# Projecting the attention branch with seven products in place of eight, and moving the weight sums into the attention heads

## The chip, the cores and the metric

The kernel runs on one core of a Trainium2 chip. The metric is device time in microseconds of one execution. The engines are PE (TensorE: matrix products, with weight loads shown as PEld), DVE (VectorE), ACT (ScalarE), POOL (GpSimd) and SP (SyncE, which here only issues transfers). The profile gives the time of every instruction on every engine.

## The reference

One layer of an encoder trunk on 1,024 rows of 1,024 columns, in float32:

```python
h = rmsnorm(x, g_mix)
z = h @ w_in                      # pooling channels | q | k | v
y_pool = pool_mixer(u_pool, w_pool_grp, pool_scale)            # (S, 512)
y_attn = diff_attention(q, k, v, g_q, g_k, lam, g_sub, ...)    # (S, 1024), 8 heads
gates = sigmoid(h @ w_gate + b_gate)                           # (S, 2048)
merged = (gates[..., :D] * (y_pool @ w_branch_pool)
          + gates[..., D:] * (y_attn @ w_branch_attn))
x = x + merged @ w_out
h2 = rmsnorm(x, g_ffn)
x = x + square(relu(h2 @ w_up)) @ w_down
```

The change concerns the two lines of `merged`, and the loading of weights for them and for `w_out`.

## The kernel before, in words

*Products in three passes.* Every float32 operand is split into a high part (a cast to fp32r on ACT) and a low part (a subtraction on DVE or POOL): `split(hi, lo, src, lo_eng)`, lines 131 and 132 in the profile. `mm3` then issues three matmuls: high x high, high x low, low x high (lines 138 to 140). Almost all matmuls of the kernel are of this kind, with up to 512 moving columns.

*Stages.* First the attention heads. A loop over `g` steps through 64 pairs of a head and a row tile (8 heads of 8 tiles of 128 rows). In one step, each of the stages A (q, k, v projection), B (preparation: norm of q and k), C (transposes), D (scores), E (transposed weights), F (product with v), H and R (norm of the output) works on a different pair, in the order of the string `O`. Stage B uses POOL for the power of the norm (`ms`, line 271) and to scale k (`qn`, line 710). Stage W loads the weights of the next head two steps before it begins, into the two buffers of `raw`, and splits them with POOL. Units of other work fill PE in between: the gate columns (`fwgate`, written to `g_dram`) and the pooling groups (written to `p_dram`). Each head writes its unscaled output to `y_dram` and one scale per row to `r_dram`. The order of the instructions on each engine is made by a scheduler that goes by the order of the program and by estimated times; each engine then works its list in order. All loads shown as SP's are issued from SP's one queue, in order.

*The branch stage.* A first loop over eight column tiles `d` projects the pooling branch (`branch_pool`: 24 matmuls; ACT copies the two halves into `mp[d]`). Beside it the same loop forms sums of blocks of `w_out` on POOL and stores them to DRAM (`w_out_sums`), and loads, scales and splits the attention output (`yT`). A second loop over `d` multiplies `mp[d]` with its gate (`gp`), projects the attention branch with 48 matmuls (`ba`, `proj_T`, both halves, eight depth tiles each), multiplies with the other gate (`ga`, result `mg`), adds it into `mp[d]` on POOL, and begins to make the left operands of the next stage (`a_set`).

*The output projection* multiplies `merged` with `w_out` as a 2 x 2 matrix of blocks by seven products in place of eight (Strassen's scheme in Winograd's form). The weight blocks come from `w_out` and from its sums in DRAM; the sums of the left operand are formed on DVE (`half(...)`). Products accumulate on one another in PSUM, named by digits: `A_RAW` says which half tile each uses. After it, the second norm and the MLP follow, whose two products use the same scheme.

*Buffers.* PSUM has eight banks; in the branch stage `ps_z` has two, `ps_f` one, `pb` five. In SBUF: `up` (tag U, 11 tiles of 128 x 1,024), `vpool` (6), `fwpool` (4), `wpool` (tags W0 and W1, 4 each), `rpool` (2 raw tiles), `fp` (`fr` and `fo`, 2 each), `fq` (one each of `fu`, `mx`), `hp0` (two times 4) and `hp1` (8).

Of the kernel before, what the change touches and what calls it, by code (L numbers as in the profile page):

```python
# [50 lines left out]
F_FROM, F_PACE, F_UNITS = 4, 0.5, 34  # L51

# [11 lines left out]
def encoder_kernel(  # L64
# [101 lines left out]
    def load_cols(src, c0, name, nk=NK):  # L166

        rw = raw([P, nk, P], f"r{name}")
        nc.sync.dma_start(rw, src[0 : nk * P, c0 : c0 + P].rearrange("(kk p) c -> p kk c", p=P))
        ws = []  # L170
        for j in range(0, nk, 4):
            w = wt([P, 2, 4, P], f"w{name}_{j}")
            split(w[:, 0], w[:, 1], rw[:, j : j + 4, :], nc.gpsimd)
            ws.append(w)
        return ws

    def load_cols2(src, c0, name):

        rw = raw([P, 4, 2 * P], f"r{name}")
        nc.sync.dma_start(rw, src[0 : 4 * P, c0 : c0 + 2 * P].rearrange("(kk p) c -> p kk c", p=P))  # L180
        ws = []
        for j in range(2):
            w = wt([P, 2, 4, P], f"w{name}_{j}")
            split(w[:, 0], w[:, 1], rw[:, :, j * P : (j + 1) * P], nc.gpsimd)
            ws.append([w])
        return ws

# [13 lines left out]
    def proj_T(ps, ws, rhs, th, nk=NK):  # L201

        for k in range(nk):
            w = ws[k // 4]
            r_hi, r_lo = rhs(k, th)
            mm3(ps, w[:, 0, k % 4, :], w[:, 1, k % 4, :], r_hi, r_lo, k == 0, k == nk - 1)
        return ps

    def load_split(src, r0, name, tile_fn, scale=None):

        rw = raw([P, S], f"r{name}") if scale is None else wt([P, S], f"r{name}", F32)
        nc.sync.dma_start(rw, src[r0 : r0 + P, :])
        if scale is not None:
            rbs, row = scale
            n = S // len(rbs)
            for i, rb in enumerate(rbs):
                js = slice(i * n, (i + 1) * n)
                nc.sync.dma_start(rb, row[js].partition_broadcast(P))
                nc.vector.scalar_tensor_tensor(rw[:, js], rw[:, js], gs, rb, op0=ALU.mult, op1=ALU.mult)
# [17 lines left out]

    def branch_pool(d, ws, ps_fn):

        m = htile([P, S], F32, f"mp{d}", 1)  # L240
        for th in range(2):
            ps = proj_T(ps_fn(f"bp{d}_{th}"), ws, lambda k, th: pair(ypT[k][th]), th, nk=4)
            nc.scalar.copy(m[:, th * 512 : (th + 1) * 512], ps)
        mp.append(m)
# [21 lines left out]
    yd = dram.tile([S, D], F32, name="yd")  # L266

# [145 lines left out]
    with ExitStack() as ph:  # L413
# [502 lines left out]

        units, made = fillers(), 0
        for g in range(-2, N + 10):
# [10 lines left out]
            if g == G_COLS:  # L929
                columns()  # L930
            gens = {}
# [40 lines left out]
    def yt_tile(d):  # L972
        fn = ut if d < N_YU else vt
        return lambda shape, dt, name, th: fn(shape, dt, name)

# [7 lines left out]
    ws_bp = {0: load_cols2(w_branch_pool, 0, "bp0")}  # L983
    ypT = [load_split(p_dram, g * P, f"ypT{g}", ypt_tile) for g in range(4)]
    mp, yT, ws_ba = [], [], {}
    w_sum = [dram.tile([S // 2, D], F32, name=f"w_sum{i}") for i in range(2)]

    def w_out_sums(d):

        b1, b2 = (vt([P, D], F32, f"wos{d}_{i}") for i in range(2))  # L990
        for i, b in enumerate((b1, b2)):
            nc.sync.dma_start(b, w_out[(d + 4 * i) * P : (d + 4 * i + 1) * P, :])
        (b11, b12), (b21, b22) = ((b[:, 0:512], b[:, 512:D]) for b in (b1, b2))
        sub(pool, b11, b12, b11)
        sub(pool, b12, b22, b12)
        sub(pool, b22, b22, b11)
        sub(pool, b21, b21, b22)
        for i, b in enumerate((b1, b2)):
            nc.sync.dma_start(w_sum[i][d * P : (d + 1) * P, :], b)

    for d in range(NK):
        if d % 2 == 0 and d + 2 < NK:
            ws_bp[d + 2] = load_cols2(w_branch_pool, (d + 2) * P, f"bp{d + 2}")
        elif d > NK - 4:
            j = len(ws_ba)
            ws_ba[j] = load_cols(w_branch_attn, j * P, f"ba{j}")
        branch_pool(d, ws_bp[d - d % 2][d % 2], bank)
        if d < 4:
            w_out_sums(d)
        if d % 4 < 2:  # L1010
            rb = [fu_tile(f"rb{d}") if d % 2 else ut([P, S], F32, f"rb{d}")]
        else:
            rb = [tmp(f"rb{d}_{i}") for i in range(2)]
        yT.append(load_split(y_dram, d * P, f"yT{d}", yt_tile(d), (rb, r_dram[d])))
    def half(d, th):
        return mp[d][:, th * 512 : (th + 1) * 512]

# [6 lines left out]
    a_sets = {}  # L1024
    for d in range(NK):
        if d + 2 < NK:
            ws_ba[d + 2] = load_cols(w_branch_attn, (d + 2) * P, f"ba{d + 2}")
# [7 lines left out]
        for th in range(2):  # L1035
# [5 lines left out]
            if th == 0:  # L1041
                a_set("1" if d < 4 else "2", d % 4)
# [576 lines left out]
```

## Time and profile before

| | |
|---|---|
| runs (median, lowest, highest) | 1529.79, 1528.99, 1529.82 us |
| span of the profiled execution | 1526.9 us |
| its own time | not given apart; the median of the runs is 2.9 us above the span |
| heads | to about 640 us |
| last gate columns | 640 to 695.7 us |
| pooling projection | 695.7 to 739.4 us |
| attention projection | 739.4 to 826.3 us |
| output projection | from 826.3 us |
| transferred | 213.75 MB, mean 140 GB/s |

A row of the groups reads: line, engine, operation, output<-inputs, shapes, xcount | busy us, mean ns of one | idle time of the engine before them, and what ended it. A row of a tile's view reads: line, engine, operation, xcount: shortest/median/longest ns, first and last start. A matmul's duration there is a modelled latency, since matmuls overlap in the array; starts are measured. A row of the waits reads: engine and line <- what ended the wait: us in total, times, longest. A row by stretches has, for each engine, its busy us and the number of its instructions, then the granted clock of TensorE, the busy share of the 16 DMA engines, and GB/s.

### The profile page before, as it was taken

How to read it: one execution, taken by the hardware profiler on the slowest of the kernel's cores; microseconds unless marked ns; L12 is line 12 of the kernel's file. 1: busy time of each engine (PE TensorE's matmuls, PEld its weight loads, DVE VectorE, ACT ScalarE, POOL GpSimd, SP SyncE). 2: the span in 40 equal slices, each digit the busy share in tenths (PEclk: the TensorE clock that was granted, in tenths of full speed). 3: DMA queues.
4: the chain of work that ended last, by engine and by line, in shares of the span. 5: the costliest groups of instructions: out<-in, count | busy, mean ns of one | idle time of the engine just before them, and what ended most of it. 6: DMA issues, size and time to landing. Idle time of an engine off the chain costs nothing.

```text
span 1526.9 us, 21743 instructions
## 1 busy us (share of the span) xinstructions
PE 1517.4 (99%) x7637; PEld 1316.2 (86%) x7637; DVE 1025.5 (67%) x2135; ACT 794.6 (52%) x1653; POOL 389.4 (26%) x466
## 2 busy tenths in 40 slices
PE   9999999999999999999999999999999999999999
PEld 8899999999999999888888887888888788888887
DVE  7877766677777777742645899676656678556672
ACT  6655555556555555544633467565555634333331
POOL 5525242434334352318646510000000000000000
PEclk9999999999999999999999999999999999999999
DMA  6212111111202021339745633554433899537650
GB/s 213 66 48 66 34 53 52 59 51 39 73 31 80 33 87 49 118 106 376 269 139 174 212 138 117 173 195 156 152 124 111 290 333 367 182 125 260 229 191 28
DMA packets 168583, 213.75 MB, mean 140 GB/s; under 512 B 10165, under 2 KB 104090, under 8 KB 168474
## 3 DMA queue, kind: packets, MB, share of 16 engines
q1 hardware_dynamic: 151050, 185.05, 36.4%
q10 hardware_dynamic: 17424, 27.31, 4.9%
q8 instruction: 60, 0.98, 0.3%
q14 instruction: 49, 0.40, 0.1%
HBM read 154.62 MB, written 57.70 MB: 139 GB/s over the span
## 4 chain that ended last, share of the span: by engine, by line
PE 96%; DVE 2%; DMA 1%; ACT 1%; issue 0%; SPq 0%; POOLq 0%; POOL 0%; ACTq 0%; DVEq 0%
PE z L138 6%; PE z L139 5%; PE z L140 5%; PE Da L139 4%; PE Da L140 4%; PE Da L138 4%; PE g L138 4%; PE g L139 4%; PE g L140 4%; PE Db L138 3%; PE Db L139 3%; PE Db L140 3%; PE X L138 3%; PE X L139 3%; PE X L140 3%; PE sc L767 2%
## 5 line engine op out<-in xcount | busy, mean ns | idle before, releaser
L138 PE MATMUL z<-wqkv,hT 128*128 128x384 f32 x512 | 173.7, 340 | 1.2 <-ACT hT L131 1.1
L140 PE MATMUL z<-wqkv,hT 128*128 128x384 f32 x512 | 173.6, 339 | 0.4 <-DVE hT L437 0.3
L139 PE MATMUL z<-wqkv,hT 128*128 128x384 f32 x512 | 173.2, 338 | 0.0
L778 ACT ACTIVATE s<-s,nm 128x256 f32<-128x256 f32 (+7 forms) x128 | 99.5, 778 | 77.6 <-DVE nm L770 74.3
L271 POOL TENSOR_TENSOR ms<-ms,mhalf 128x4 f32<-128x4 f32 x64 | 66.7, 1042 | 186.8 <-DVE ms L270 183.3
L138 PE MATMUL g<-hT,fwgate 128*128 128x512 f32 x256 | 101.0, 395 | 0.0
L139 PE MATMUL g<-hT,fwgate 128*128 128x512 f32 x256 | 100.5, 392 | 0.0
L140 PE MATMUL g<-hT,fwgate 128*128 128x512 f32 x256 | 100.4, 393 | 0.0
L138 PEld LDWEIGHTS z<-wqkv,hT 128*128 128x128 f32 x512 | 96.2, 188 | 4.0 <-ACT hT L131 1.2
L140 PEld LDWEIGHTS z<-wqkv,hT 128*128 128x128 f32 x512 | 96.2, 188 | 2.6 <-DVE hT L437 0.9
L139 PEld LDWEIGHTS z<-wqkv,hT 128*128 128x128 f32 x512 | 96.3, 188 | 2.4 <-DVE wqkv L437 0.3
L770 DVE CUSTOM_DVE_ANT_0 s<-sc,dist 128x512 f32<-128x512 f32 (+3 forms) x128 | 74.1, 585 | 21.2 <-PE sc L768 20.3
L767 PE MATMUL sc<-K,Q 128*128 128x512 f32 (+2 forms) x192 | 67.5, 357 | 0.4 <-DVE nm L770 0.4
L768 PE MATMUL sc<-K,Q 128*128 128x512 f32 (+2 forms) x192 | 66.1, 349 | 0.0
L132 DVE TENSOR_TENSOR AS<-s,AS 128x512 fp32r<-128x512 f32 x64 | 43.4, 687 | 30.9 <-ACT AS L131 30.9
L132 POOL TENSOR_TENSOR wqkv<-rqkv,wqkv 128x384 fp32r<-128x384 f32 x56 | 58.7, 1065 | 14.6 <-ACT wqkv L131 14.2
L132 POOL TENSOR_TENSOR fwgate<-frgate,fwgate 128x512 fp32r<-128x512 f32 x32 | 43.5, 1361 | 66.0 <-ACT fwgate L131 66.0
L140 PEld LDWEIGHTS g<-hT,fwgate 128*128 128x128 f32 x256 | 48.1, 188 | 9.5
L138 PEld LDWEIGHTS g<-hT,fwgate 128*128 128x128 f32 x256 | 48.1, 188 | 9.1 <-ACT go L387 0.2
L139 PEld LDWEIGHTS g<-hT,fwgate 128*128 128x128 f32 x256 | 48.1, 188 | 8.8
L132 DVE TENSOR_TENSOR AT_0l<-ta,AT_0h 128x512 fp32r<-128x512 f32 (+1 forms) x48 | 32.0, 666 | 32.0 <-ACT AT_0h L131 31.7
L139 PE MATMUL ba<-yT,wba 128*128 128x512 f32 x128 | 49.6, 389 | 0.0
(481 smaller groups left out, 4625.9 us busy)
## 6 DMA issues: line engine op xcount, KB each, us to landing
wd<-in_w_down_dram SPq DMA_DIRECT2D x56, 512.0 KB, 5.4
wu<-in_w_up_dram SPq DMA_DIRECT2D x32, 512.0 KB, 4.3
udS<-us SPq DMA_DIRECT2D x64, 256.0 KB, 3.3
ur<-udS SPq DMA_DIRECT2D x32, 512.0 KB, 4.5
rqkv<-in_w_in_dram SPq DMA_DIRECT2D x64, 192.0 KB, 3.0
ur<-ud SPq DMA_DIRECT2D x24, 512.0 KB, 6.4
frgate<-in_w_gate_dram SPq DMA_DIRECT2D x32, 256.0 KB, 3.6
g_dram<-go ACTq DMA_DIRECT2D x32, 256.0 KB, 3.2
```

The lines of the kernel that those rows point to most:

```text
L132: (lo_eng or nc.vector).tensor_tensor(lo, src, f(hi), op=ALU.subtract)
L138: nc.tensor.matmul(ps, lhs_hi, rhs_hi, start=first, stop=False, **kw)
L139: nc.tensor.matmul(ps, lhs_hi, rhs_lo, start=False, stop=False, **kw)
L140: return nc.tensor.matmul(ps, lhs_lo, rhs_hi, start=False, stop=last, **kw)
L271: nc.gpsimd.tensor_tensor(dst, dst, mhalf[:, :n], op=ALU.pow)
L767: nc.tensor.matmul(dst, Q[:, i, 0, :], rhs, start=True, stop=False)
L768: nc.tensor.matmul(dst, Q[:, i, 1, :], rhs, start=False, stop=True)
L770: nc.vector.tensor_tensor_reduce(out=s[i][:, c : c + w], in0=sc[:, 0:w], in1=dist[:, o0 + c : o0 + c + w], scale=2.0 ** -(h + 1), scalar=B ...
L778: nc.scalar.activation(s[i][:, 0:n], s[i][:, 0:n], AF.Exp, bias=last, scale=-1.0, accum_out=Z[:, i, t : t + 1])
```

## The change

- The attention branch is projected by seven products on 2 x 2 blocks (512 x 512), in the order `1265734`, with operands named as in the output projection. The weight blocks come from `w_branch_attn` and from its sums in DRAM; the sums of y are formed on DVE. y is loaded whole and scaled (`load_y`), and split for each product (`by_set`, low part on DVE); the weights are loaded and split for each product (`wa_set`, low part on POOL). Some partial results are copied out of PSUM by ACT, others are added on DVE; `merge` multiplies with the gate on DVE and adds into `mp` on POOL (the last product: on DVE).
- The sums of `w_branch_attn` and `w_out` are formed by POOL during the heads: 16 calls of `weight_sums`, each on 128 x 256 columns of four blocks, in the steps `g` of 8 or more whose remainder by 8 is 1, 3 or 5, ahead of the step's stages. They go through `raw` tiles and SP's queue. The old `w_out_sums` goes.
- The pooling branch (`gated_pool`) loads its gate first; DVE multiplies straight out of PSUM into `mp`, in place of ACT's copy and a later multiplication.
- The column loaders and `proj_T` go; the order of the loads around the branch changes with it.

The diff, without the removed helpers and a few tile functions:

```diff
+SUM_FROM, SUM_T = 8, (1, 3, 5)
...
+    w_sum = {n: [dram.tile([S // 2, D], F32, name=f"{n}_sum{i}") for i in range(2)] for n in "ao"}
...
+        def weight_sums(n, d, c):
+            src, eng = w_branch_attn if n == "a" else w_out, nc.gpsimd
+            r = raw([P, 4, 256], f"ws{n}{d}_{c}")
+            def rows_of(t, d):
+                return t[d * P : (d + 1) * P, :].rearrange("p (j c) -> p j c", j=2)[:, :, c * 256 : (c + 1) * 256]
+            for i in range(2):
+                nc.sync.dma_start(r[:, 2 * i : 2 * i + 2, :], rows_of(src, d + 4 * i))
+            b11, b12, b21, b22 = (r[:, i, :] for i in range(4))
+            def put(op, out_, a, b):
+                eng.tensor_tensor(out_, a, b, op=op)
+            if n == "a":
+                put(ALU.add, b22, b12, b22)
+                put(ALU.subtract, b12, b11, b12)
+                put(ALU.subtract, b11, b22, b11)
+                put(ALU.subtract, b21, b21, b11)
+            else:
...
+            for i in range(2):
+                nc.sync.dma_start(rows_of(w_sum[n][i], d), r[:, 2 * i : 2 * i + 2, :])
+        sums = [(n, d, c) for n in "ao" for d in range(4) for c in range(2)]
...
+            if g % 8 in SUM_T and sums and g >= SUM_FROM:
+                weight_sums(*sums.pop(0))
...
-    def w_out_sums(d):
...
-    for d in range(NK):
-        if d % 2 == 0 and d + 2 < NK:
-            ws_bp[d + 2] = load_cols2(w_branch_pool, (d + 2) * P, f"bp{d + 2}")
-        elif d > NK - 4:
-            j = len(ws_ba)
-            ws_ba[j] = load_cols(w_branch_attn, j * P, f"ba{j}")
-        branch_pool(d, ws_bp[d - d % 2][d % 2], bank)
-        if d < 4:
-            w_out_sums(d)
-        ...
-        yT.append(load_split(y_dram, d * P, f"yT{d}", yt_tile(d), (rb, r_dram[d])))
+    def gated_pool(d):
+        gp = gate_tile(f"gp{d}", d)
+        gate(whole(gp)[0], d)
+        mp.append(htile([P, S], F32, f"mp{d}", 1))
+        w = ws_bp.pop(d)
+        for th in range(2):
+            ps = bank(f"bp{d}_{th}")
+            for k in range(4):
+                mm3(ps, w[:, 0, k, :], w[:, 1, k, :], *pair(ypT[k][th]), k == 0, k == 3)
+            nc.vector.tensor_tensor(half(d, th), ps, gp[:, th * 512 : (th + 1) * 512], op=ALU.mult)
+    def load_y(d):
+        t = ut([P, S], F32, f"yr{d}")
+        nc.sync.dma_start(t, y_dram[d * P : (d + 1) * P, :])
+        for i in range(2):
+            js = slice(i * 512, (i + 1) * 512)
+            rb = tmp(f"rb{d}_{i}")
+            nc.sync.dma_start(rb, r_dram[d][js].partition_broadcast(P))
+            nc.vector.scalar_tensor_tensor(t[:, js], t[:, js], gs, rb, op0=ALU.mult, op1=ALU.mult)
+        yr.append(t)
...
+    B_ORDER = "1265734"
+    def wa_set(j):          # W tiles, tag by the parity of the product's place
...
+            wa[j] += load_rows(
+                src, (d0 + d) * P, dh * 512, f"a{j}_{d}", lambda shape, name: w_tile(shape, name, n % 2)
+            )
+    def by_set(j):
+        n = B_ORDER.index(j)
+        by_[j] = []
+        for d in range(4):
+            t = (fw_tile if n % 2 else lambda shape, name: vt(shape, F32R, name))([P, 2, 512], f"by{j}_{d}")
+            split(t[:, 0, :], t[:, 1, :], BY[j](d))
+            by_[j].append(t)
+    def b_product(ps, j, i):
+        c = slice(i * P, (i + 1) * P)
+        for d in range(4):
+            mm3(
+                ps, wa[j][d][:, 0, c], wa[j][d][:, 1, c], *pair(by_[j][d]),
+                j in "125" and d == 0, d == 3, j not in "125",
+            )
+    def merge(d, th, k, eng):
+        ga = tmp(f"ga{d}_{th}")
+        gate([(ga, th * 512, (th + 1) * 512)], NK + d)
+        out_ = ga if k.space == PSUM else k
+        nc.vector.tensor_tensor(out_, k, ga, op=ALU.mult)
+        add(eng, half(d, th), half(d, th), out_)
...
-    for d in range(NK):
...
-            ps = proj_T(bank(f"ba{d}_{th}"), ws, lambda k, th: pair(yT[k][th]), th)
-            mg = tmp(f"mg{d}_{th}")
-            nc.vector.tensor_tensor(mg, ps, ga[:, hs], op=ALU.mult)
-            add(pool, half(d, th), mg, half(d, th))
...
+    load_bp(0)
     for d in range(NK):
+        if d % 2 == 0 and d + 2 < NK:
+            load_bp(d + 2)
+        gated_pool(d)
+        load_y(d)
+        if d == 3:
+            wa_set("1")
+            by_set("1")
+            for e in range(4):
+                sub(dve, yh(e, 0), yh(e, 1), yh(e, 0))
+    wa_set("2")
+    by_set("2")
+    for d in range(4):
+        sub(dve, t2(d), yh(d + 4, 1), yh(d, 0))
+        sub(dve, yh(d + 4, 0), yh(d + 4, 0), t2(d))
+        sub(dve, yh(d, 1), yh(d + 4, 1), yh(d, 1))
+    X = [pb.tile([P, 512], F32, tag="b", name=f"bX{i}") for i in range(4)]
+    x1 = kept4("bx1")
+    for i in range(4):
+        b_product(X[i], "1", i)
+        nc.scalar.copy(x1[i], X[i])
+    wa_set("6")
+    by_set("6")
+    Y = [o_bank(f"bY{i}", i) for i in range(4)]
+    for i in range(4):
+        b_product(Y[i], "2", i)
+        add(dve, x1[i], Y[i], x1[i])
+        merge(i, 0, x1[i], pool)
+        a_set("1", i)
+    wa_set("5")
+    by_set("5")
+    U2 = kept4("bU2")
+    for i in range(4):
+        b_product(X[i], "6", i)
+        nc.scalar.copy(U2[i], X[i])
+    wa_set("7")
+    by_set("7")
+    Z = [o_bank(f"bZ{i}", i) for i in range(4)]
+    z5 = kept4("bz5")
+    for i in range(4):
+        b_product(Z[i], "5", i)
+        nc.scalar.copy(z5[i], Z[i])
+    wa_set("3")
+    by_set("3")
+    for i in range(4):
+        b_product(X[i], "7", i)
+        add(dve, z5[i], X[i], z5[i])
+        merge(i + 4, 1, z5[i], pool)
+    wa_set("4")
+    by_set("4")
+    for i in range(4):
+        b_product(Z[i], "3", i)
+        add(dve, U2[i], Z[i], U2[i])
+        merge(i, 1, U2[i], pool)
+        add(dve, half(i, 1), half(i, 1), half(i + 4, 1))
+        sub(dve, half(i, 0), half(i, 1), half(i, 0))
+    for i in range(4):
+        b_product(X[i], "4", i)
+        merge(i + 4, 0, X[i], dve)
+        a_set("2", i)
+        sub(dve, half(i + 4, 0), half(i + 4, 0), half(i, 0))
```

More of the change, by code (lines that the diff above doesn't have):

```diff
@@ L164, in fu_tile @@
         return fq.tile([P, S], F32, tag="fu", name=name)
[L166 to L186, printed above, removed]
     loads = {}
```

110 lines of the change are left out of this document (46 added, 64 removed).

## The prediction, made before the changed kernel was run

> **What bounds the kernel now.** I read the page's busy times and chain first, then who PE waited for, then the busy times stage by stage, and last the rows of the two projections.
>
> ```profile
> span 1526.9 us, 21743 instructions
> PE 1517.4 (99%) x7637; PEld 1316.2 (86%) x7637; DVE 1025.5 (67%) x2135; ACT 794.6 (52%) x1653; POOL 389.4 (26%) x466
> PE 96%; DVE 2%; DMA 1%; ACT 1%; issue 0%; SPq 0%; POOLq 0%; POOL 0%; ACTq 0%; DVEq 0%
> ...
> PE z L138 <- ACT hT L131: 1.1, 1, 1.1
> PE sc L767 <- DVE nm L770: 0.4, 1, 0.4
> ```
>
> The third line is the chain: 96% of it is PE. The last two are everything that PE waited for between 40 and 930 us (engine, line, releaser; total us, times, longest). Heads, branch stage and output projection together hold 1.5 us of waiting, so a matmul taken away there is worth its whole time, and any wait put there costs its whole time.
>
> ```profile
> core 0: us, PE busy (x) PEld busy (x) DVE busy (x) ACT busy (x) POOL busy (x), PEclk, DMA share, GB/s
> 120.00:640.00 520.00, 519.55 (x3021) 479.99 (x3020) 377.74 (x1136) 298.32 (x773) 201.62 (x277) 1.00 0.19 59
> 640.00:695.70 55.70, 55.70 (x281) 47.05 (x280) 25.05 (x61) 26.54 (x50) 10.86 (x12) 1.00 0.40 134
> 695.70:739.40 43.70, 43.70 (x194) 36.21 (x193) 16.44 (x16) 19.90 (x36) 38.30 (x28) 1.00 1.04 394
> 739.40:826.30 86.90, 86.90 (x385) 71.94 (x384) 44.41 (x52) 38.06 (x56) 49.91 (x36) 1.00 0.46 144
> 826.30:880.60 54.30, 54.30 (x241) 44.98 (x240) 41.60 (x54) 24.29 (x50) 32.01 (x23) 1.00 0.70 236
> ```
>
> The rows are the heads, the last gate columns, the pooling projection, the attention projection, and most of the output projection. The granted clock is 1.00 throughout. The output projection matters most as a witness: it already runs seven products with the same splits, and PE never waits in it. In the pooling row the DMA engines are full (1.04).
>
> ```profile
> 739.43 0.39 PE L138 MATMUL ba<-yT,wba 128*128 128x512 f32 x1
> ...
> 826.24 0.39 PE L140 MATMUL ba<-yT,wba 128*128 128x512 f32 x1
> L138 PE MATMUL ba<-yT,wba x128: 389/389/389, 739.4 to 825.8; 128*128 128x512 f32 x128
> L1039 DVE TENSOR_TENSOR mg<-ba,ga x16: 676/682/693, 749.8 to 830.1; 128x512 f32<-128x512 f32 x16
> ```
>
> The attention projection is 3 x 128 = 384 matmuls. Their starts run from 739.43 to 826.24 us, 86.81 us for 383 steps: one starts every 0.2267 us. The 389 ns are a latency, not a price.
>
> **The change, part by part.**
>
> (1) Seven products of 4 row tiles x 4 depth tiles x 3 passes are 336 matmuls of the same shape; 48 fall away: 48 x 0.2267 = 10.9 us, all on the path. One product is 48 matmuls, also 10.9 us, and that is the time base below. The pooling projection keeps its 192.
>
> (2) What the products ask of the other engines. The rows:
>
> ```profile
> L131 ACT CAST A<-mp x28: 602/616/625, 753.4 to 883.2; 128x512 fp32r<-128x512 f32 x28
> L132 DVE TENSOR_TENSOR A<-mp,A x28: 675/932/1777, 754.0 to 886.3; 128x512 fp32r<-128x512 f32 x28
> L243 ACT COPY mp<-bp x16: 580/587/589, 701.4 to 739.6; 128x512 f32<-128x512 f32 x16
> L1032 DVE TENSOR_TENSOR mp<-mp,gp x16: 681/694/1799, 746.5 to 786.0; 128x512 f32<-128x512 f32 x16
> L230 ACT ACTIVATE gp<-gp,zero x16: 706/724/726, 745.7 to 784.9; 128x512 f32<-128x512 f32 x16
> L132 DVE TENSOR_TENSOR A<-mp,A 128x512 fp32r<-128x512 f32 x21 | 22.1, 1063 | 6.2 <-ACT A L131 6.2
> L132 POOL TENSOR_TENSOR wo<-ro,wo 128x512 fp32r<-128x512 f32 x28 | 41.7, 1507 | 26.3 <-ACT wo L131 15.6 <-PE oX L138 6.0 <-PE oX L140 2.9
> L948 POOL TENSOR_TENSOR mp<-mg,mp x16: 1287/1300/1759, 750.6 to 831.3; 128x512 f32<-128x512 f32 x16
> ```
>
> Each product needs four weight tiles (cast on ACT, low part on POOL) and four y tiles (cast on ACT, low part on DVE). That is ACT 8 x 0.62 = 4.9 us, POOL 4 x 1.51 = 6.0 us, DVE 4 x about 0.95 = 3.8 us. A DVE operation with both inputs in SBUF has a floor of 0.68 and a mean of 1.06 beside a busy POOL (the row with 1063); 0.95 lies by the median of the second row. From PSUM it is 0.68. Buffers are double by product (four tiles of one kind, then four of the other), so a set can be made while the product before it runs: 6.0 us of work in 10.9.
>
> A merging product (2, 7, 3 of the order 1-2-6-5-7-3-4) adds four sigmoids (2.9 ACT), four PSUM sums and four gate multiplies (2.7 + 3.8 DVE) and four POOL additions (5.2). The heaviest is product 2, which also makes the first output-projection set: ACT 4.9 + 2.9 + 2.5 = 10.3, DVE 3.8 + 6.5 + 3.8 = 14.1, POOL 11.2, in 10.9 us. It overruns by 3 us, and the next two products (DVE 3.8 each, POOL 6.0, ACT 4.9 + 4 x 0.587 = 7.2) give it back. Cost 0; a copy out of PSUM has another product between it and the bank's next use, 10.9 us of cover.
>
> The end is the tight place.
>
> ```profile
> 820.80 1.77 DVE L948 TENSOR_TENSOR mp<-mp,mp 128x512 f32<-128x512 f32 x1 [1.84 <-POOL mp L948]
> 822.60 1.67 DVE L951 TENSOR_TENSOR mp<-mp 128x512 f32<-128x512 f32 x1
> 824.06 3.07 POOL L132 TENSOR_TENSOR wo<-ro,wo 128x512 fp32r<-128x512 f32 x2 [0.34 <-ACT wo L131]
> 824.30 1.67 DVE L951 TENSOR_TENSOR mp<-mp,mp 128x512 f32<-128x512 f32 x1
> ```
>
> Where DVE and POOL both read SBUF without a pause, an operation takes DVE 1.7 us and POOL 1.5. Products 7, 3 and 4 give DVE 8 y splits, 8 PSUM sums, 8 multiplies, 8 half sums, then 4 PSUM multiplies, 4 additions, 4 splits of the second output set and 4 subtractions: 12 from PSUM, 36 from SBUF. POOL has 20: 8 weight tiles, 8 additions, 4 tiles of the first output set. At the floor DVE needs 48 x 0.68 = 32.6 us, exactly the 32.6 us of three products, and is not late. With the overlap: 12 x 0.68 = 8.2 us beside which POOL does 6 alone; 14 meet, 14 x 1.7 = 23.8; 22 alone, 15.0; in all 47.0 us, 14.4 late. The last split is first read 10.9 + 9 x 0.2267 = 12.9 us after the branch ends. So PE waits 0 to 1.5 us for it, and up to 4 us more where the later sets pass the delay on (DVE is idle 54.3 - 41.6 = 12.7 us in the output projection and takes it up). Taken: 1.5 us, the reading that counts the overlap.
>
> The Trainium skill, SBUF — State Buffer, Who interferes with whom, says that a DVE instruction with two SBUF inputs contends with a GpSimd instruction that reads SBUF, over a shared port that it calls an exclusive lock. By that rule the two would run strictly one after the other, 0.68 + 1.29 = 1.97 us a meeting (the shortest of each), 50.8 us in all, and the sum would be 3.8 us higher. The rows above disagree in part: a meeting costs DVE 1.7, not 1.97.
>
> (3) The pooling branch. Sixteen ACT copies (16 x 0.587 = 9.4 us) go, and the sixteen multiplies become reads of PSUM: same count, 0.68 in place of 0.69 to 1.80. The gates come before, not after, the projection: eight sigmoids of 1,024 columns must be done between 690 and 735 us. Eight PSUM banks stand between PE and the first multiply, 12 matmuls each, so DVE may be 8 x 2.7 = 21.8 us late. Cost 0; without the banks, one load and one sigmoid, about 4 us, once.
>
> (4) y. It is scaled once and kept whole; before, it was split as a whole.
>
> ```profile
> 740.38 2.43 DVE L219 SCALAR_TENSOR_TENSOR ryT<-ryT,gs,rb 128x512 f32<-128x512 f32 x2
> rb<-r_dram SPq DMA_DIRECT2D x8, 256.0 KB, 7.6
> rqkv<-in_w_in_dram SPq DMA_DIRECT2D x64, 192.0 KB, 3.0
> frgate<-in_w_gate_dram SPq DMA_DIRECT2D x32, 256.0 KB, 3.6
> ```
>
> The last head's rows were scaled only at 740 to 743 us, behind full DMA engines. In the new order product 2 is the first to want them, at 739.4 + 10.9 = 750, and product 6 the sums, at 761. The twelve differences cost 12 x 0.95 = 11.4 us of DVE under the pooling row (16.4 of 43.7 busy). The 8 MB of output-weight sums leave that row, and 4 MB of gates enter it. Cost 0, with 7 us of cover.
>
> (5) The weight sums in the heads: 16 sums, each with two loads and two stores of 256 KB on SP and four POOL operations of 128x256.
>
> ```profile
> L271 POOL TENSOR_TENSOR ms<-ms,mhalf 128x4 f32<-128x4 f32 x64 | 66.7, 1042 | 186.8 <-DVE ms L270 183.3 <-DVE cf L785 3.1
> L132 POOL TENSOR_TENSOR wqkv<-rqkv,wqkv 128x384 fp32r<-128x384 f32 x56 | 58.7, 1065 | 14.6 <-ACT wqkv L131 14.2
> L710 POOL TENSOR_TENSOR qn<-qn,ggh 128x128 f32<-128x128 f32 x64 | 35.4, 553 | 55.5 <-DVE qn L704 46.3 <-DVE ms L270 5.3 <-DVE cf L785 2.4
> L138 PE MATMUL z<-wqkv,hT x512: 331/334/446, 8.9 to 615.8; 128*128 128x384 f32 x171
> L435 SPq DMA_DIRECT2D rqkv<-in_w_in_dram x56: 367/451/1463, 14.7 to 540.0; - x56
> udS<-us SPq DMA_DIRECT2D x64, 256.0 KB, 3.3
> SPq L312 <- POOL fwgate L132: 230.7, 26, 34.2
> ```
>
> The trace has no 128x256 operation on POOL: it lies between 128x128 (0.55) and 128x384 (1.07), 0.81 us, so 64 cost 52 us. POOL is idle 520 - 201.6 = 318 us in the heads, so they fit.
>
> What stands behind them matters more: the power of the norm (ms) and the scaling of k on POOL, and the weight loads on SP. A step of the heads lasts (615.8 - 8.9) / 64 = 9.5 us. The sums stand in the odd steps of a head, where POOL prepares a row tile of even number, which is turned with its odd neighbour two steps later. Four operations, 3.2 us, or those and a load of 3.6 us in front of them, stay under that 19 us. On SP, 64 more issues at 0.45 us are 29 us, and a store waits for its sums, with weight and gate loads queued behind; SP already stands 230.7 us on gate buffers, so loads run ahead. The two raw buffers are shared with the next head's weights; a sum holds one for 3.6 (load) + 3.2 + 3.3 (store) = 10 us, and those weights are wanted 19 us after the last sum of a head. Bounds on PE: 0, and 16 x (3.6 + 3.2) = 109 us if each sum were exposed. Taken: 0, because nothing in the waits shows POOL as what PE waited for.
>
> (6) Gone from the pooling row: the old sums.
>
> ```profile
> L951 POOL TENSOR_TENSOR wos<-wos 128x512 f32<-128x512 f32 x8 | 11.9, 1505 | 0.1
> L951 POOL TENSOR_TENSOR wos<-wos,wos 128x512 f32<-128x512 f32 x8 | 10.7, 1346 | 0.2
> ```
>
> These 22.6 us of POOL free nothing that PE waits for: POOL worked 38.3 of 43.7 us there, and PE did not wait. Worth 0.
>
> **Sum.** The median of the runs is 1529.79, 2.9 us above the profiled span. 1526.9 - 10.9 + 1.5 + 2.9 = 1520.4 us.
>
> **The rivals.**
>
> A. DVE becomes the bound at the branch's end, and passes it on. For it: 47 us of work in 32.6, and two more stages behind it that want DVE. If each meeting costs 0.68 + 1.29 = 1.97 us, one after the other, or the sets of the next products come late in turn, 3 to 7.6 us come back: 1521.9 to 1526.5, still faster. Against: the output projection, where DVE's SBUF operations already averaged 1.06 and PE waited for none.
>
> By the rule of the Trainium skill named above the heads would pay too, and even then 377.7 + 52 of their 520 us would leave DVE idle time.
>
> B. The handovers eat the gain. The pooling row's DMA stays full, the y rows come over 7 us late, and products 2 and 6 wait: 8 to 14 us come back, 1526.9 to 1532.9, no change. Against: 8 MB leave that row.
>
> C. The sums hold POOL, and the heads wait: slower. Their four operations (or the load ahead of them) stand before the norm's power in its only queue, the transposes come late, and PE idles once per sum. It decides from 10.9 / 16 = 0.7 us per sum. One uncovered sum operation and part of the next, 1.2 us each, give 1520.4 + 19 = 1539. For it: ms is the commonest thing on POOL, and the chain through it is short. Against: POOL itself waited for DVE there (183.3 us).
>
> **How the numbers follow.** A change under 0.2% (3.1 us) is about what a measurement of this kernel cannot tell. Forecast 0.55, A 0.26, B 0.09, C 0.10. Forecast and A are faster, B is the same, C slower. The forecast alone spans 1517.6 (no wait: the fastest run, 1528.99, less 10.9 and 0.5 of the old waits) to 1521.9; the range takes in A and the edge of B and leaves out the rest: 1517.6 to 1526.5.
>
> **What would show it.** 7,589 matmuls; 528 branch matmuls 0.2267 us apart, within about 120 us; PE's waits in the heads as before (C shows as PE behind ms or qn); ms still about 1.0 us; product 2 and the second product of the output projection without a wait (A shows there, as PE behind the split of A); POOL at about 250 us in the heads. I am wrong if PE waits over 8 us in any of these places.

## The result and the profile after

The changed kernel takes 1539.01 us (median of 4 runs, 1537.66 to 1540.30) against 1529.80 us before in the same comparison: 1.0058 times the time, 95% interval 1.0044 to 1.0073. It is 9.2 us slower; 9.4 us faster were forecast. Its profiled execution took 1539.02 us, with a span of 1537.2. The page:

```profile
span 1537.2 us, 21914 instructions
PE 1514.8 (99%) x7589; PEld 1309.7 (85%) x7589; DVE 1078.3 (70%) x2183; ACT 801.7 (52%) x1671; POOL 434.3 (28%) x520
...
PE 81%; DVE 7%; DMA 4%; POOL 3%; issue 2%; ACT 1%; SPq 0%; POOLq 0%; ACTq 0%; DVEq 0%
```

The 48 matmuls are gone (7637 to 7589), and the share of PE in the chain fell from 96% to 81%: other engines now set the pace in places. Who PE waited for between 40 and 930 us:

```profile
PE oX L139 <- DVE mp L936: 2.6, 2, 1.6
PE bp L139 <- ACT wbp L132: 2.3, 1, 2.3
PE ta L780 <- DVE s L744: 1.9, 2, 1.0
PE bp L139 <- ACT rT L840: 1.6, 1, 1.6
PE trr L838 <- POOL r L836: 1.5, 1, 1.5
PE oY L139 <- ACT A L132: 1.3, 1, 1.3
PE z L139 <- ACT hT L132: 1.1, 1, 1.1
PE X L139 <- ACT y L1252: 0.9, 1, 0.9
PE oX L140 <- POOL wo L133: 0.7, 1, 0.7
PE oZ L139 <- DVE nrs L227: 0.6, 1, 0.6
PE oY L141 <- DVE A L133: 0.4, 1, 0.4
```

1.5 us of waits became 14.9. The new ones lie at three places: the heads (ta), the entry to the pooling projection (bp, and trr, the transposition of the last head's scale rows), and the output projection (oY, oX), with 1.5 us more behind them (oZ, X). By stretches, with the columns of the rows before the change (heads, last gates, pooling projection, the seven products, the output projection up to oZ):

```profile
120.00:640.00 520.00, 518.13 (x3015) 478.59 (x3014) 381.18 (x1134) 294.25 (x769) 240.28 (x326) 1.00 0.26 82
640.00:702.60 62.60, 58.77 (x292) 48.80 (x290) 27.85 (x63) 28.39 (x51) 10.66 (x10) 1.00 0.58 185
702.60:750.60 48.00, 46.40 (x193) 37.84 (x194) 36.73 (x47) 20.62 (x32) 19.82 (x14) 0.93 0.63 208
750.60:826.70 76.10, 76.10 (x337) 63.04 (x336) 60.22 (x56) 40.59 (x72) 56.61 (x38) 1.00 0.50 164
826.70:889.30 62.60, 57.61 (x242) 45.74 (x242) 51.19 (x62) 29.93 (x59) 41.10 (x27) 0.97 0.58 185
```

The fourth row is the forecast gain: 336 matmuls in 76.1 us, dense. The second, the third and the fifth hold most of the loss, and the granted clock, 1.00 everywhere before, is 0.93 in the third and 0.97 in the fifth. The boundaries come from the first rows of the tiles:

```profile
L139 PE MATMUL z<-wqkv,hT x512: 331/334/444, 9.5 to 618.9; 128*128 128x384 f32 x171
L139 PE MATMUL bp<-ypT,wbp x64: 389/389/792, 702.6 to 749.9; 128*128 128x512 f32 x64
L139 PE MATMUL bX<-by,wa x64: 389/389/389, 750.6 to 826.1; 128*128 128x512 f32 x64
L139 PE MATMUL oX<-wo,A x64: 388/389/470, 826.7 to 888.6; 128*128 128x512 f32 x64
```

From such rows, stage by stage, for every kernel run (us; of the profiled execution, whose time lies up to 2 us off the median, in e8, e10 and e11 4.1, 2.8 and 2.4):

| kernel | median | ratio to before, interval | last z at | to first product (ba, bX) | products, to first oX | oX to oZ | rest of span |
|---|---|---|---|---|---|---|---|
| before | 1529.8 | | 615.8 | 123.6 | 87.1 | 54.4 | 646.0 |
| changed | 1539.0 | 1.0058 (1.0044-1.0073) | 618.9 | 131.7 | 76.1 | 62.6 | 647.9 |
| e1 y later | 1536.2 | 1.0042 (1.0027-1.0057) | 618.5 | 126.0 | 77.9 | 63.2 | 648.3 |
| e2 no sums | 1537.7 | 1.0054 (1.0039-1.0069) | 616.1 | 129.4 | 76.2 | 64.3 | 648.4 |
| e3 before + sums | 1532.7 | 1.0020 (1.0011-1.0030) | 618.2 | 123.6 | 87.0 | 54.4 | 646.6 |
| e4 light merge | 1534.2 | 1.0031 (1.0018-1.0044) | 618.1 | 130.5 | 76.1 | 59.3 | 648.2 |
| e5 wu early | 1537.7 | 1.0050 (1.0035-1.0065) | 620.3 | 130.7 | 76.2 | 63.7 | 646.4 |
| e6 sums after qn | 1536.9 | 1.0043 (1.0029-1.0057) | 616.0 | 130.2 | 76.1 | 65.8 | 647.6 |
| e7 PSUM merge | 1537.7 | 1.0051 (1.0036-1.0066) | 619.0 | 130.0 | 76.2 | 63.5 | 647.9 |
| e8 combined | 1527.8 | 0.9991 (0.9982-1.0000) | 616.5 | 126.8 | 77.9 | 60.9 | 647.9 |
| e9 4 before 3 | 1542.7 | 1.0087 (1.0071-1.0102) | 617.3 | 130.4 | 76.3 | 66.9 | 649.4 |
| e10 e8 + e9 | 1531.9 | 1.0019 (1.0010-1.0028) | 616.5 | 126.6 | 77.7 | 60.2 | 651.8 |
| e11 e10 + 8 on POOL | 1536.0 | 1.0041 (1.0029-1.0054) | 616.0 | 128.1 | 76.2 | 58.7 | 652.8 |
| e12 no half sums | 1534.3 | 1.0031 (1.0019-1.0043) | 619.0 | 130.6 | 76.1 | 59.1 | 647.3 |
| e13 gate part alone | 1529.5 | 1.0000 (0.9991-1.0009) | 616.1 | 123.6 | 87.0 | 54.4 | 646.3 |
| e14 e8 + 4 on POOL | 1529.1 | 1.0000 (0.9992-1.0009) | 615.8 | 125.6 | 77.6 | 61.4 | 646.1 |

The first two rows are the account: +3.1 heads (0.6 of it a later start), +8.1 entry and pooling projection, -11.0 products, +8.2 output projection, +1.9 after it (1.5 of them the waits at oZ and X): +10.3 us of span.

### The profile page after: what moved, and what is told of

Its sections match the earlier page's. It is cut to its first block, busy times and chain, and to the rows that moved or that the text cites. A ratio compares the mean times of both kernels' runs of the same rounds, so it can differ in the third digit from the quotient of the medians.

```text
span 1537.2 us, 21914 instructions
## 1 busy us (share of the span) xinstructions
PE 1514.8 (99%) x7589; PEld 1309.7 (85%) x7589; DVE 1078.3 (70%) x2183; ACT 801.7 (52%) x1671; POOL 434.3 (28%) x520
## 4 chain that ended last, share of the span: by engine, by line
PE 81%; DVE 7%; DMA 4%; POOL 3%; issue 2%; ACT 1%; SPq 0%; POOLq 0%; ACTq 0%; DVEq 0%
PE z L141 5%; PE z L140 5%; PE z L139 5%; PE Da L140 4%; PE Da L141 4%; PE Da L139 4%; PE Db L140 3%; PE Db L139 3%; PE Db L141 3%; PE g L139 3%; PE g L140 3%; PE g L141 3%; PE X L139 3%; PE X L140 3%; PE X L141 3%
## 5 line engine op out<-in xcount | busy, mean ns | idle before, releaser
L133 POOL TENSOR_TENSOR wa<-ra,wa 128x512 fp32r<-128x512 f32 x28 | 43.2, 1561 | 32.2 <-ACT wa L132 29.9
```

What stands on the lines that cost most here:

```text
L133: (lo_eng or nc.vector).tensor_tensor(lo, src, f(hi), op=ALU.subtract)
```

## The experiments

### The heads: what the sums cost

In the changed kernel POOL's list around 245 us reads (start, us, instruction, idle before it and what ended that):

```profile
245.01 0.74 POOL L887 TENSOR_TENSOR wso<-wso 128x256 f32<-128x256 f32 x1 [2.10 <-DMA wso<-in_w_out_dram]
246.58 1.55 POOL L887 TENSOR_TENSOR wso<-wso 128x256 f32<-128x256 f32 x2 [0.83 <-DMA wso<-in_w_out_dram]
248.09 1.01 POOL L228 TENSOR_TENSOR ms<-ms,mhalf 128x4 f32<-128x4 f32 x1
```

and DVE's:

```profile
249.13 0.42 DVE L661 TENSOR_TENSOR qn<-z,ms 128x256 f32<-128x256 f32 x1 [3.05 <-POOL ms L228]
249.47 0.28 DVE L133 TENSOR_TENSOR AT<-ta,AT 128x128 fp32r<-128x128 f32 x1
249.67 1.00 DVE L744 SCALAR_TENSOR_TENSOR s<-s,cf,s 128x768 f32<-128x768 f32 x1
```

A sum stood at the head of POOL's queue until its transfer had landed, with the norm's power behind it; DVE waited 3.05 us for that power, with `s` behind it; PE then waited 0.9 us for `s`. That is rival C's mechanism, once in this clear form rather than sixteen times. At the second wait (1.0 us at 410 us) two sums had stood 3.29 and 0.76 us for their transfers, but DVE waited only 0.73 us for the power, and `s` itself took 2.02 us in place of the 1.18 of e2 and e6, beside POOL's splits of gate weights.

**e2**, the sums left out:

```diff
-            if g % 8 in SUM_T and sums and g >= SUM_FROM:
-                weight_sums(*sums.pop(0))
```

> The changed kernel without the weight sums; blocks of the two weights themselves are loaded in their place (their values are not the reference's), so loads and splits of the projections stay as they are. If POOL's sums in the heads cost what the lag of the projections' starts shows (0.6 us before step 4, not theirs, then 2.45 us in two jumps): the last head's projection starts 2.4 us earlier, and the time is about 1536.5. If the sums also cause the rest (their stores, their transfers): 1530 or below. If they cost nothing on the chip: 1539.

Measured: 1537.71 us. The ta waits are gone and the last z is at 616.1, 2.8 us earlier and as in the kernel before. The median fell by 1.3 us, less than the 2.5 expected; the output projection of the profiled execution took 1.7 us longer. Four runs between 1536.20 and 1539.80 do not tell 1.3 from 2.5.

**e3**, the kernel before with the 16 sums in its heads:

```diff
+            if g % 8 in SUM_T and sums and g >= SUM_FROM:
+                weight_sums(*sums.pop(0))
...
-        if d < 4:
-            w_out_sums(d)
```

> The kernel before, with all 16 weight sums of both weights in the heads as in the change and the old sums left out; the sums of the attention weights are not used. If the heads' loss is the sums' own: the heads end 2 to 3 us later and the time is 1531.5 to 1533. If the loss needs the new branch stage: 1529.8. If taking the old sums out of the pooling row is worth something: under 1529.

Measured: 1532.69 us. All of it is in the heads (last z 618.2; every other stage within 0.6 us of before). The sums, with the old ones taken out, cost 3.0 us (1532.69 - 1529.73, the median before in that comparison; interval 1.7 to 4.6).

**e6**, the same sums, their arithmetic pinned behind the next step's last POOL operation of stage B:

```diff
+            q_done[0] = nc.gpsimd.tensor_tensor(qn[:, 2:4, :], ...)   # stage B
...
             def put(op, out_, a, b):
-                eng.tensor_tensor(out_, a, b, op=op)
+                with tc.issue_after(q_done[0].ins):     # called one step after the loads
+                    eng.tensor_tensor(out_, a, b, op=op)
```

> Each weight sum's four GpSimd operations are moved: loads as before, arithmetic issued one step later and right behind that step's last GpSimd operation of the q,k preparation. Theory (a queue wait): the 2.5 us by which the heads got longer come from sums that stand at the head of GpSimd's queue until their transfer has landed (2.10 us at 245), ahead of the power of ms on which DVE waits. Then the last z starts at about 616.5 instead of 618.9 us, and the time is 1536.7 (1536 to 1537.3), since nothing later has slack for it. Rival (port contention of GpSimd's sums with DVE, or the sums' DMA traffic): the last z stays at 618 or later and the time at 1538.5 or more.

Measured: 1536.91 us. Every wait of PE between 40 and 640 us that is left in e6, and the row of z:

```profile
PE z L139 <- ACT hT L132: 1.1, 1, 1.1
L139 PE MATMUL z<-wqkv,hT x512: 331/334/444, 8.7 to 616.0; 128*128 128x384 f32 x171
```

The same 64 operations and 64 transfers now cost the heads 607.3 - 606.9 = 0.4 us in place of 2.5. Both waits are gone. So it was the place in the queue, not the amount of POOL's work, the sums' meeting with DVE at the port, or the traffic. The time fell by 2.1 us, as the theory has it, though the output projection of the profiled execution took 65.8.

### The entry: y's rows

DVE's list in the changed kernel, before the pooling projection:

```profile
676.35 1.72 DVE L1009 SCALAR_TENSOR_TENSOR yr<-yr,gs,rb 128x512 f32<-128x512 f32 x1 [5.39 <-DMA rb<-r_dram]
...
689.61 0.75 DVE L1009 SCALAR_TENSOR_TENSOR yr<-yr,gs,rb 128x512 f32<-128x512 f32 x1 [1.97 <-DMA rb<-r_dram]
690.28 0.28 DVE L820 CUSTOM_DVE_ANT_0 oq<-po,identf 128x128 f32<-128x128 f32 x1
...
690.70 1.29 DVE L133 TENSOR_TENSOR ypT<-rypT,ypT 128x512 fp32r<-128x512 f32 x2
```

Scalings of y stand in front and wait for rows (`rb`). Behind them are the last head's sum of squares and the splits of the pooling operands, which free the raw tiles for the weights of bp. PE idles 2.3 and 1.6 us, and then starts a matmul every 0.43 us:

```profile
702.60 0.50 PE L139 MATMUL bp<-ypT,wbp 128*128 128x512 f32 x1 [2.30 <-ACT wbp L132]
...
705.41 0.79 PE L139 MATMUL bp<-ypT,wbp 128*128 128x512 f32 x1 [1.60 <-ACT rT L840]
706.00 0.63 PE L140 MATMUL bp<-ypT,wbp 128*128 128x512 f32 x1
706.43 0.63 PE L141 MATMUL bp<-ypT,wbp 128*128 128x512 f32 x1
```

**e1**, y's scaling behind the last low part of `ypT`:

```diff
+            with tc.issue_after(ypT_done.ins):
                 nc.sync.dma_start(rb, r_dram[d][js].partition_broadcast(P))
                 nc.vector.scalar_tensor_tensor(t[:, js], t[:, js], gs, rb, ...)
```

> The changed kernel, with the scale rows and the scaling of y held behind the last split of the pooling rows. If DVE's queue, held by scalings that wait for their scale rows, is what made the pooling projection start at 702.6 and run 47.8 us instead of 43.5: the projection starts within 1 us of the last gate column (about 699), runs 43.5 us, and the time falls by 6 to 8 us, to about 1532. If the load of its weights is late for another reason (full transfer queues, or POOL): it still starts about 3 us after the last gate column and the time stays within 2 us of 1539. If the y rows are what the branch cannot wait for: products 2 and 6 wait and the time rises.

Measured: 1536.25 us. From the last z to the first product it takes 126.0 in place of 131.7 us, and the pooling projection starts 0.6 us after the last gate column in place of 3.1. But the time falls by 2.8 us, not by 6 to 8. DVE now has y's work inside the pooling projection, and a gate multiply (L1003) comes late for the first product; further on, an add (L938) comes late in the output projection:

```profile
PE oX L141 <- DVE mp L938: 3.4, 1, 3.4
PE bX L141 <- DVE mp L1003: 1.9, 1, 1.9
```

The wait of bX lies ahead of the first product, inside the 126.0. Half of the 5.7 us is given back later: 1.8 in the products, where no wait is left but 7 starts behind that of bX lie 0.426 us apart, and 1.0 behind them.

**e13**, the pooling gate part alone on the kernel before:

```diff
-            nc.scalar.copy(m[:, th * 512 : (th + 1) * 512], ps)
+            nc.vector.tensor_tensor(m[:, th * 512 : (th + 1) * 512], ps, gp[th], op=ALU.mult)
```

> The kernel before with one part of the change alone: the pooling branch's products are gated straight out of PSUM by DVE (no copies on ACT, no later multiply), with its gate rows loaded and put through the sigmoid in the pooling projection. Theory (the prediction's third step): within 0.5 us of the kernel before, 1529.8, since eight banks cover the gates. Rival (the gate rows share SP's queue and the small tiles with y's rows, so that banks come free late): 1532 or more, with PE waiting for DVE's multiply in or behind the pooling projection.

Measured: 1529.54 us, ratio 1.0000, every stage within 0.3 us. By itself, on the kernel before, this part costs nothing and brings nothing.

### The end of the branch and the output projection

DVE in the changed kernel is busy without a gap from before 826 to 846 us; the last row is POOL's at the same time:

```profile
836.34 1.78 DVE L939 TENSOR_TENSOR mp<-mp,mp 128x512 f32<-128x512 f32 x1
838.04 0.68 DVE L1065 TENSOR_TENSOR ga<-bX,ga 128x512 f32<-128x512 f32 x1
838.64 1.18 DVE L133 TENSOR_TENSOR A<-mp,A 128x512 fp32r<-128x512 f32 x1
839.74 1.77 DVE L936 TENSOR_TENSOR mp<-mp,ga 128x512 f32<-128x512 f32 x1
...
842.64 0.67 DVE L133 TENSOR_TENSOR A<-mp,A 128x512 fp32r<-128x512 f32 x1
...
834.27 6.70 POOL L133 TENSOR_TENSOR wo<-ro,wo 128x512 fp32r<-128x512 f32 x4 [4.32 <-issue]
```

The merges of the branch's last product are still under way 13 us after PE has left the branch, and the last split of the second operand set starts at 842.64, 15.9 us after it; the forecast had DVE 14.4 us late.

**e4**, the 12 gate multiplies with both inputs in SBUF left out:

```diff
-        nc.vector.tensor_tensor(out_, k, ga, op=ALU.mult)
+        if k.space == PSUM:
+            nc.vector.tensor_tensor(out_, k, ga, op=ALU.mult)
```

> The changed kernel with 12 of the 16 multiplications with the attention gate left out (those whose two inputs are in SBUF; the gates are still loaded and made). If DVE's lag at the end of the branch is what makes the output projection wait: 8 to 20 us of DVE work go, the second output product no longer waits for its left operand, the granted clock stays at 1.00 between 838 and 849 us, and the time falls by 6 to 9 us, to 1530 to 1533. If the weights split by POOL are late: the waits stay and the time stays within 2 us of 1539.

Measured: 1534.15 us. The waits in oY are gone and oX to oZ takes 59.3 in place of 62.6; one wait at oX, 2.7 us, stays, and the time falls by 4.9 us, less than the 6 to 9 of the theory.

**e12**, the 12 half sums left out:

```diff
-        add(dve, half(i, 1), half(i, 1), half(i + 4, 1))
-        sub(dve, half(i, 0), half(i, 1), half(i, 0))
...
-        sub(dve, half(i + 4, 0), half(i + 4, 0), half(i, 0))
```

> The changed kernel without the 12 half sums of the combined branch (the adds and differences of mp's halves after products 3 and 4); the later operand sets are split from the unsummed halves, so this part of the result is left out. Theory (rival A of the prediction: DVE's work and its contention with GpSimd from the branch's last products on make the output projection's operands and its adds late): the waits at oX after 855 us (2.6 us) go, the stretch from the first oX to the first oZ comes from 62.6 to 58 or less, time 1534.5 (1533 to 1536). Rival (the two raw tiles: the loads of the output projection's weights wait for GpSimd's splits, ACT waits for them, and DVE behind): the stretch stays at 61.5 or more and the time at 1538 or more.

Measured: 1534.33 us, oX to oZ 59.1. Its stretch, and the wait at oX, which the theory had gone:

```profile
825.70:884.80 59.10, 56.29 (x241) 46.05 (x240) 45.31 (x55) 30.73 (x61) 38.45 (x27) 0.97 0.63 199
PE oX L139 <- DVE mp L936: 2.8, 1, 2.8
```

Two different cuts in DVE's work at the branch's end give 4.9 and 4.7 us in the time, 3.3 and 3.5 of them in this stretch: DVE's work is the cause of about 3.4 of the 8.2 us. The rest is mostly the wait that neither removes and the lower clock behind it (0.97 in the row).

**e5**, the first MLP weights released earlier, since DVE stood 3.2 us at 853 us for one of them with all of this behind it:

```diff
-                    later.enter_context(tc.issue_after(loads["o5"].ins))
+                    later.enter_context(tc.issue_after(loads["o2"].ins))
```

> The loads of the first MLP weights (wu) are released by the output projection's load o2 instead of o5, so that they no longer stand in SP's queue behind the four loads from the summed w_out, which wait for POOL's splits. Theory (an order on SP and DVE): in the changed kernel DVE stood 3.24 us at 853-856 for a wu transfer, with the adds of oY and the splits of the next operand sets behind it, and PE then waited 2.6 us for the adds of oX at 864 and 876, on a lower clock. Then DVE's wait and most of the 2.6 us go, the stretch from the first oX to the first oZ comes down from 62.6 us to about 59, and the time from 1539.0 to 1535.5 (1534 to 1536.5). Rival (DVE is late from the branch's end, and the wu transfer is only what the profile names): the stretch stays at 61.5 or more and the time at 1538.5 or more.

Measured: 1537.73 us, between the two forecasts, and a stretch of 63.7, as the rival has it. DVE's wait is gone, and PE waits for something else:

```profile
PE oX L139 <- ACT A L132: 3.1, 1, 3.1
```

**e7**, products 2 and 3 merged in PSUM, half sums after the splits of set 2:

```diff
-        add(dve, x1[i], Y[i], x1[i])
-        merge(i, 0, x1[i], pool)
+        add(dve, Y[i], Y[i], x1[i])
+        merge(i, 0, Y[i], pool)
```

> Products 2 and 3 of the branch are summed with their kept copies in place in PSUM, so that 8 of the 12 gate multiplies read PSUM instead of two SBUF operands, and the half sums of products 3 and 4 come after the splits of operand set 2. Nothing is left out. Theory (DVE's end work and its contention with GpSimd delay set 2): the second operand set's splits come 2 to 4 us earlier, the 1.7 us that PE waits before and in oY go, and the time is 1537 (1536 to 1538). Rival A': the wait at oX stays, since it hangs on SP's order, and takes back all of it: 1538.5 to 1539.5. Rival B': the deferred half sums are now late for set 6 and the first oX of product 6 waits: 1540 or more.

Measured: 1537.71 us, inside the theory's range, but not by its mechanism: the waits in oY (2.2) and oX (2.7) stay and the stretch is 63.5, as rival A' has it. What the profiled execution gains lies ahead of the edit, and 1.3 us is less than such kernels differ from run to run.

**e9**, product 4 ahead of product 3:

```diff
-    B_ORDER = "1265734"
+    B_ORDER = "1265743"
...
-    U2 = kept4("bU2")
+    U2 = [t2(i) for i in range(4)]
```

> The changed kernel with its last two branch products exchanged (4 ahead of 3) and product 6's copies kept in the tiles of y's third sum, so that their room in the first operand pool is free. The merges of product 4, and with them the splits of the output projection's second operand set, then lie one product (10.9 us) further from the branch's end; what ends last is product 3, which the later sets need two products later. Theory (the end is the tight place, as the prediction's second step had it): the 1.7 us of waits in oY and the clock that falls after them go, the stretch from the first oX to the first oZ comes down from 62.6 to 59 or less, the time to 1536 (1534.5 to 1537). Rival (DVE is late by its total work, whatever the order): the waits move to oX's third and fourth product, the stretch stays at 61.5 or more and the time at 1538 or more.

Measured: 1542.68 us, slower by another 3.7. The waits in oY go, as the theory has it, and waits at oX of 7.9 and 1.9 us take their place, as the rival has it: the half sums now fall beside POOL's splits of the output weights.

```profile
861.03 5.10 DVE L939 TENSOR_TENSOR mp<-mp,mp 128x512 f32<-128x512 f32 x3
```

Three of them, 1.7 us each, in a row in front of the adds that PE waits for. Here DVE's lateness is a debt that the order moved and did not remove.

### All mends together

**e8**: e1, e5, e6 and e7 in one kernel.

> All four mends together: y's scaling behind the last low split of ypT (which gave 2.8 us alone), sums behind qn, products 2 and 3 merged in PSUM with the half sums late, and wu released by o2. Theory (separate losses in series): heads -2.3, entry -2.8, branch end -1.5, output projection -3.5, together 1529 (1527.5 to 1531). Rival (shared waits: DVE is the bound through the whole branch and a loss removed at one place comes back at the next): 1533 or more, with DVE at 10 of 10 us in the pooling projection and with bX and oX still waiting for DVE. Faster than the kernel before only if it comes under 1528.

Measured: 1527.81 us (10 runs), 11.2 less than the changed kernel; ratio to before 0.9991, interval 0.9982 to 1.0000. That is inside the theory's range, and by the interval not shown to be faster than the kernel before. The four alone add up to 2.8 + 1.3 + 2.1 + 1.3 = 7.5, each known to some 2 us, so the difference to 11.2 is not shown to be one. The longest waits of PE that are left in e8, from an execution of 1531.92 us, the slowest of the ten:

```profile
PE bX L141 <- DVE mp L1010: 3.0, 1, 3.0
PE oY L141 <- ACT A L134: 1.8, 1, 1.8
PE oY L143 <- DVE A L135: 1.6, 1, 1.6
```

**e10**, e8 with e9's order, and **e11**, e10 with 8 of y's 16 differences on POOL; **e14**, e8 with 4 of them on POOL:

```diff
-        sub(dve, yh(d, 1), yh(d + 4, 1), yh(d, 1))
+        sub(pool, yh(d, 1), yh(d + 4, 1), yh(d, 1))
```

> The four mends of the combined version, and the exchange of products 4 and 3 with product 6's copies in the tiles of y's third sum. Combined so far: first oX at 821.2, first oZ at 882.1, 60.9 us where dense work takes 54.4, with 3.4 us of waits in oY for the second operand set. Theory (that set's lateness): the oY waits go and the stretch comes to 56 (54.5 to 57.5), the time from 1527.8 to 1523 (1521.5 to 1525). Rival (DVE's work is only moved): stretch 60 or more, time 1527 or more.

> As the run before, and 8 of the 16 differences of y's quarters on GpSimd instead of DVE in the pooling projection. Theory (DVE's work there is what makes the gate multiplies late, so that bX finds its banks taken): the 3.0 us that bX waits and the lower clock behind it go, 3 us less than the run before (2 to 4). Rival (GpSimd's longer operations and the shared port give back as much; the gate rows' tiles, of which there are two, set the multiplies' pace): within 1 us of the run before.

> The combined version (1527.8) with 4 of the 16 differences of y's quarters on GpSimd: the ones that product 7 reads, which are not ahead of the splits of the pooling projection's weights as the 8 of the run before were (bp waited 3.1 us for those). Theory (DVE's work delays the gate multiplies and so bX): of the 3.0 us that bX waits 1 to 3 go, time 1525.5 (1524.5 to 1527). Rival (the round of two gate tiles sets the pace, or GpSimd's share of the port gives it back): 1527.5 or more.

Measured: 1531.86, 1536.04 and 1529.12 us. In e10 the oY waits go, the stretch gains 0.7, and the rest of the span loses 3.9, 1.05 of them in a wait of oZ for a DVE sum: part of the debt is paid after the first oZ. In e11 bX waits for nothing, but bp waits 3.1 us for its weights' splits, which alternate with the differences in POOL's list. In e14 bX still waits 2.5 us in place of 3.0. In e10 and e14 the rivals held, in e11 neither. e8 stays the best version, ahead of the kernel before by at most 0.2%, if at all.

## Why the prediction was wrong, point by point

The forecast was 1520.4 us and the median 1539.0, 18.6 us apart. By the stages that is 3.1 in the heads, 8.1 up to the first product, 6.7 in the output projection (8.2 less the 1.5 taken) and 1.9 after it, less 0.1 in the products and 1.1 because the median lies 1.8 and not 2.9 us above the profiled span.

1. *Step (1), 10.9 us from 48 matmuls*: right. 336 matmuls took 76.1 us without a wait.
2. *Step (2), the engine work of the products*: right inside the branch (no wait at bX, bY, bZ), and at its end right in place and nearly in size: waits in oY of 1.7 us against 1.5 taken. The term that failed is the other half of the same sentence, "up to 4 us more where the later sets pass the delay on", of which nothing was taken because DVE is idle 12.7 us in the output projection. That idle time did not take the delay up: in the changed kernel the stretch has 9.6 us more of DVE's work (51.2 in place of 41.6), and DVE is still idle for 11.4 of its 62.6 us, 6.2 of them, as before, in waits for ACT's casts. The stretch lost 8.2 us, 3.3 and 3.5 of them given back by e4 and e12. The rest is waits and clock; neither e5 (the order of SP's loads) nor e7 (the place of the sums) shortened the stretch, and its cause stays open.
3. *Step (3), gates at no cost*: right by itself (e13). With y's work beside it, in e1 and e8, PE waits 1.9 and 3.0 us for such a multiply ahead of the first product.
4. *Step (4), y at no cost with 7 us of cover*: wrong. The cover was counted from when the products want y. What was not counted is what stands behind y's scaling on DVE: the last head's chain and the pooling operands. The step also counts twelve differences of y, where the diff has sixteen (four more at `d == 3`). e1 gives back 5.7 us of the 8.1 there, and 2.8 in the time.
5. *Step (5), sums at no cost*: wrong by 3.0 us (e3). The step named the danger, "those and a load of 3.6 us in front of them", and set 19 us of slack against it. That slack belongs to k's transposes; the same DVE list also holds `s`, the two softmaxes of a head combined, which at the first wait was held from 246.1 to 249.7 us and had 2.7 of these 3.6 us to spare, PE waiting for the last 0.9. Rival C had the mechanism and 6 times the price: that its 1539 us is the measured time is luck, since it puts 19 us into the heads, which lost 3, and nothing at the other two places.
6. *Step (6), the old sums worth nothing*: right as far as seen; e3 drops them and its pooling projection is unchanged.
7. *"Any wait put there costs its whole time"*: too low a price. The sum has no term for the clock, and behind two waits of 3.9 us together the entry lost 2.0 us more (the last section).

Rival A, with its passing on, was the nearest in mechanism, but its 1526.5 us ends where two further losses begin. The sum treated three costs of order as covered (the passing on, y, the sums), each by a stretch of time that was real; for y and the sums it belonged to another instruction of the same queue.

## What to carry to other kernels

Slack belongs to an instruction, not to an engine: before an operation that waits for a transfer is put into an in-order queue at no cost, look up the instruction behind it and when that one's reader wants it. Where sums are needed late, pin them behind the last urgent operation of a step (e6: 0.4 us in place of 2.5). And a matmul saved at the price of vector work is only saved if the engine that does that work is not late at the seam that follows.

## What the runs showed of the hardware

In these runs a wait often cost more than its length. After 2.3 and 1.6 us of idle time at 700 to 705 us the starts of matmuls lay 0.426 us apart for 10 steps (the rows at 706.00 and 706.43), against 0.2267 otherwise: 2.0 us lost on top of 3.9. At 841 to 843 us waits of 1.3 and 0.4 us were followed by 7 such steps, 1.4 us lost on top of 1.7; single waits of 0.9 to 1.6 us (heads, oX at 864) by none, single ones of 1.9 to 3.4 us in e1 and e12 by 5 to 7. The length alone does not decide: a wait of 1.9 us in e9 (oX at 848) was followed by none, waits of 1.5 and 0.3 us in e11 (936 to 937) by 8, and the same two in e10 by none. The profiled executions without waits of PE beyond 1.1 us between 40 and 930 us (before, e3, e13) had a mean granted clock of 1.000, the others 0.994 to 0.998. The Trainium skill, TensorE: Matmul & The Clock Gate, Part 1, gives 426.7 ns between starts at 512 columns on the gated half-rate clock, which the trace agrees with; it puts the drop after an idle window of about 3.4 us, while here 1.7 us in all was enough at one place.

Beside POOL's splits, DVE's operations with two SBUF inputs took up to 1.78 us (836.34), with POOL's at 1.7 each (four in 6.70 us). The Trainium skill, SBUF — State Buffer, Who interferes with whom, calls the shared port an exclusive lock; one operation of each alone takes 0.68 + 1.29 = 1.97 us, so these rows stay below that rule, as the forecast had it.

Not expected: the changed kernels scatter more, run to run, than the kernel before (e8 1527.40 to 1531.92 in 10 runs, e10 1530.20 to 1536.30 in 11; before 1528.61 to 1530.41 in 23 runs of one comparison, 1529.00 to 1531.85 in 14 of another). Why was not tried.
